# Conv block on one core: where the row chunks, the taps and the sums stand in the convolution stage

## The chip, the core and the metric

The kernel runs on one core of a Trainium2 chip. Its time is the device time in microseconds of one execution; several executions are timed and the median is given. Five engines work in order, each on its own queue of instructions, and wait for each other by semaphores: TensorE (PE; its weight loads are PEld), VectorE (DVE), ScalarE (ACT), GpSimd (POOL) and SyncE (SP), which here issues the DMAs.

## The reference

One layer of a decoder with a convolution mixer, batch 1, T = 256 tokens, D = 2048 channels, an MLP of 8192, all float32.

```python
mod = silu(c) @ mod_w + mod_b                     # 6 vectors of D: sh1, sc1, g1, sh2, sc2, g2
h = rms_norm(x, norm1_g) * (1 + sc1) + sh1
u = h @ w_in + b_in                               # 2048 -> 4096
a, gt = split(u, 2)
u = a * sigmoid(gt)                               # the gate
u = causal_depthwise_conv(u, dw_w, 31 taps) + dw_b
u = silu(layer_norm(u, ln_g, ln_b))
x = x + (1 + g1) * (u @ w_out + b_out)
h = rms_norm(x, norm2_g) * (1 + sc2) + sh2
x = x + (1 + g2) * (square(relu(h @ mlp_w1)) @ mlp_w2)
```

## The kernel before

Channels lie on the 128 partitions, tokens on the free axis: D is KT = 16 tiles of 128 channels by 256 tokens. Every weight of a product is split into a high and a low part (`split_w`: ScalarE writes `hi`, L206, GpSimd or VectorE writes `lo`, L209), and a product is the sum of high x high, high x low and low x high.

**Jobs.** The work of TensorE is a list of jobs: 16 of the input product ("in", one tile of `a` and one of `gt` each), then "out", "up" and "down". The first eight input jobs are computed together while the modulation vectors are loaded and worked out. Jobs 8 to 15 then run one by one: 64 matrix instructions each into a PSUM buffer "mm", of which there are two (job 15 has 96 in another form). These jobs and what stands beside them are the convolution stage, and it is all that the change touches. Per job n in it:

- `evac` (L518 on ScalarE, L519 on VectorE) adds the two halves of the sums; `gate` (L750 sigmoid on ScalarE, L752 on VectorE) writes the gated tile `u[n]`. With that the "mm" buffer is free for a later job.
- *The convolution* of a tile goes one of two ways. Eight tiles (`PE_TILES`) go to TensorE: ScalarE, and for two of them VectorE, makes shifted copies ("wide", L710 and L712), GpSimd a diagonal of taps ("diag", L720), and `pe_conv` issues 32 small matrix instructions (L735) into an "mm" buffer of their own. `CONV_AT` says behind which job which tile comes. The other eight tiles go to VectorE: 31 instructions per tile (L621 to L627, "taps") and a join (L630). `stream` is a generator over all of them that lets the end of one tile's taps alternate with the beginning of the next one's, and `advance(k)` issues the next k steps; `ADVANCE` says how many behind which job.
- *Row chunks.* Part of the modulation comes as rows: `mod_chunk` takes one loaded weight block of 1 MB and issues four matrix instructions (L310) into the PSUM bank "row". Jobs 8 to 12 have four chunks each, job 13 three (`LATE_IN`). `mod_finish` folds a finished row sum into columns (L357) and adds the bias (L348).
- *Shift and sums.* Behind tile 1, `find_shift` (L410, L670) takes a shift from the first two tiles; later tiles start from it and `add_shift` (L674) adds it to the earlier ones. `stats(b)` squares four tiles on ScalarE (L462) and sums them and their squares on TensorE (L680), for the layer norm.

**What sets the order.** The program is written in one sequence, and a scheduler places each engine's instructions by its own estimate of when they are ready, with `urgent()` for those that go first. `tc.issue_after(x)` says that an instruction stands behind x in that order. Loads are issued by `top_up` in a fixed order as buffers come free: seven buffers "raw" hold the blocks of 1 MB of all kinds. In the version before, the row chunks of a job come behind its products and ahead of its convolution tile, the tile behind the last chunk (`step_end`), and nothing orders the next job's products against either. The taps of `advance` are not ordered against the job's gate.

Of the kernel before, what the change touches and what calls it, by code (L numbers as in the profile page):

```python
# [17 lines left out]
KT = D // P  # L18
# [23 lines left out]
FIRST = 4  # L42
PE_TILES = (0, 1, 2, 9, 10, 12, 14, 15)
CONV_AT = {9: (0,), 10: (1,), 11: (2,), 12: (9,), 13: (10,), 14: (12,), 15: (14,)}
ADVANCE = {7: 24, 8: 34, 9: 34, 10: 34, 11: 34, 12: 32, 13: 37, 14: 99}
SHIFT = 2
COPY_AT = {8: 0, 9: 1, 10: 2, 11: 9, 12: 10, 13: 12}
PADDING = 720
# [18 lines left out]
def conv_block(ctx: ExitStack, tc: tile.TileContext, x, vec, dwq, c_row, mod_r, mod_c, w_first, w_in, w_out, w1, w2, out):  # L67
    nc = tc.nc
# [15 lines left out]
    def col(name, j=0, n=1):  # L84
        at = VEC[name] + j
        return v[:, at : at + n]
# [23 lines left out]
    for i in range(2):  # L110
        p = ps.tile([P, 2, 2 * T], F32, name="mm", bufs=2)
# [6 lines left out]
    state = {"used": 0}  # L118
# [12 lines left out]
    def urgent():  # L131
        return tc.high_priority(offset=URGENT)
# [89 lines left out]
    def mm(p, c, key, acts_of, ks=range(KT), merged=False):  # L222
        halves = parts[key]
        for k in ks:
            hi, lo = halves[k // HALF]
            m = acts_of[k // 2][:, k % 2, :]
            if merged:
                out_p, begin, end = p[:, c, 0:T], k == 0, k == KT - 1
                w = hi[:, k % HALF, :]
                nc.tensor.matmul(out_p, w, m[:, 0:T], start=begin, stop=False)  # L230
                nc.tensor.matmul(out_p, w, m[:, T : 2 * T], start=False, stop=False)  # L231
                state["mm_end"] = nc.tensor.matmul(out_p, lo[:, k % HALF, :], m[:, 0:T], start=False, stop=end)  # L232
                continue
            nc.tensor.matmul(p[:, c, :], hi[:, k % HALF, :], m, start=(k == 0), stop=(k == KT - 1))  # L234
            state["mm_end"] = nc.tensor.matmul(  # L235
                p[:, c, T : 2 * T], lo[:, k % HALF, :], m[:, 0:T], start=False, stop=(k == KT - 1),
                skip_group_check=True,
            )
# [101 lines left out]
    def mod_bias(at, n, src):  # L340
        cs = slice(at, at + n)
        which, k = divmod(at, KT)
        if which in amps:
            g = col("n1g" if which == SC1 else "n2g", k, n)
            nc.vector.tensor_tensor(src, src, col("modb", at, n), op=ALU.add)
            nc.vector.tensor_tensor(amps[which][:, k : k + n], src, g, op=ALU.mult)
        else:
            return nc.vector.tensor_tensor(modc[:, cs], src, col("modb", at, n), op=ALU.add)  # L348

    def mod_finish():  # L350
        while pending:
            ats, nj, r = pending.pop(0)
            n = len(ats)
            p = ps.tile([P, 512], F32, name="row", bufs=1)
            with urgent():
                for j in range(nj):
                    state["fold_end"] = nc.tensor.matmul(  # L357
                        p[:, n * j : n * j + n], r[:, j * P : (j + 1) * P], col("pick", 0, n), start=True, stop=True
                    )
                for b, at in enumerate(ats):  # L360
                    with tc.issue_after(state["lo_end"]) if "lo_end" in state else ExitStack():
                        mod_bias(at, nj, p[:, 0 : nj * n].rearrange("p (j n) -> p n j", n=n)[:, b, :])
# [35 lines left out]
    def mods(keys):  # L398
        for key in keys:
            if key[0] == "mod":  # L400
                mod_chunk(*key[1:])
            else:
                mod_col(key[1])
# [28 lines left out]
    def two():  # L432
        return tmp.tile([P, 2, T], F32, name="two", bufs=6)
# [9 lines left out]
    hl = [None] * HALF  # L443
# [34 lines left out]
    for job in jobs:  # L478
        n = quota.get(job, 0)
# [3 lines left out]
        if job[:2] in LATE_GATE:  # L483
            n = LATE_GATE[job[:2]][job[2]]
# [39 lines left out]
    p = ps.tile([P, 512], F32, name="small", bufs=1)  # L524
# [10 lines left out]
    with urgent():  # L535
        part = two()[:, 0, :]
        nc.scalar.activation(part, p[:, 0:T], AF.Copy)
        p = ps.tile([P, 512], F32, name="row", bufs=1)
# [8 lines left out]
    for _ in range(2):  # L547
        p = ps.tile([P, 2, 2 * T], F32, name="mm", bufs=2)
# [31 lines left out]
    for k in range(KT):  # L580
        c = k % 2
# [3 lines left out]
        if c == 0:  # L585
            n = two()
# [20 lines left out]
    def cv(k):  # L607
        return cvs[k // 4][:, k % 4, :]
# [9 lines left out]
    def tap(out, acc, ct, j):  # L618
        s, w = tap_of(ct, j)
        if j == 0:  # L620
            nc.vector.tensor_scalar(out, s, w, col("dwb", ct), op0=ALU.mult, op1=ALU.add)  # L621
        elif acc is None and ct < UNSHIFTED:
            nc.vector.tensor_scalar(out, s, w, None, op0=ALU.mult)
        elif acc is None:
            nc.vector.scalar_tensor_tensor(out, s, w, state["small"][:, T : 2 * T], op0=ALU.mult, op1=ALU.add)
        else:
            nc.vector.scalar_tensor_tensor(out, s, w, acc, op0=ALU.mult, op1=ALU.add)  # L627

    def join(out, acc, s):
        nc.vector.tensor_tensor(out, acc, s, op=ALU.add)  # L630

    def conv_steps(ct):
        acc = ps.tile([P, 2, T], F32, name="acc", bufs=2)
        rest = cp.tile([P, T], F32, name="rest", bufs=2)
        for j in range(TAPS):
            n = j % 2
            tap(rest if j == TAPS - 1 else acc[:, n, :], None if j < 2 else acc[:, n, :], ct, j)
            yield
        join(cv(ct), acc[:, 1, :], rest)

    on_dve = [ct for ct in range(KT) if ct not in PE_TILES]

    def stream():
        tail = iter(())
        for ct in on_dve:
            steps = conv_steps(ct)
            for _ in range((TAPS - 1) // 2):
                next(steps)
                yield
                if next(tail, tail) is not tail:  # L650
                    yield
            for _ in tail:
                yield
            tail = steps
        for _ in tail:
            yield

    conv_taps = stream()

    def advance(n):  # L660
        for _ in range(n):
            next(conv_taps, None)
# [21 lines left out]
    def stats(b):  # L684
        s = squares(cvs[b])
        for k in range(2):
            sum_round([(cv(4 * b + 2 * m + k), s[:, 2 * m + k, :]) for m in range(2)], b == 0 and k == 0)
# [60 lines left out]
    def gate(i, t2):  # L748
        sg = two()[:, 0, :]
        state["sg"] = nc.scalar.activation(sg, t2[:, 1, :], AF.Sigmoid, bias=col("b_in", KT + i))  # L750
        u[i] = ubufs[i % len(ubufs)]
        nc.vector.scalar_tensor_tensor(  # L752
            u[i][:, PAD : PAD + T], t2[:, 0, :], col("b_in", i), sg, op0=ALU.add, op1=ALU.mult
        )
        return sg

    def mix(ct):
# [4 lines left out]
    with urgent():  # L762
# [10 lines left out]
        gate(7, held[7])  # L773
    advance(ADVANCE[HELD - 1])

    for n, job in enumerate(jobs):
# [14 lines left out]
        kind, i = job[0], job[-1]  # L791
        if kind == "out" and i > 0:
            p = ps_two()
        elif not by_tokens(job):
            p = ps.tile([P, 2, 2 * T], F32, name="mm", bufs=2)
# [3 lines left out]
        if job == ("up", 0, 0):  # L799
            mm(p, 0, job + (0,), xa, range(SIDE))  # L800
            for at in range(2 * UNSCALED):
                shift_row(at, shown.pop(("up", 0, at // 2, at % 2)))
            fold_shift()
            mm(p, 0, job + (0,), xa, range(SIDE, KT))
            mm(p, 1, job + (1,), xa)
        elif job in K_OUTER:
            for k2 in range(HALF):
                for c in range(2):
                    mm(p, c, job + (c,), xa if plain else hl, range(2 * k2, 2 * k2 + 2), kind == "out")
        elif kind == "in":  # L810
            rows = [key for key in after[job] if key not in cols_in] if i < KT - 1 else []
            for c in range(2) if i < KT - 1 else (1, 0):
                for ks in (range(HALF), range(HALF, KT)):
                    mm(p, c, job + (c,), hl, ks, i == KT - 1)
            state["step_end"] = state["mm_end"]
            with tc.issue_after(state["mm_end"].ins):
                mods(rows)
            if rows:
                state["step_end"] = state["row_end"]
        elif by_tokens(job):  # L820
            mm_tokens(sums[kind, i // 2], job, u2 if kind == "down" else hl, n == len(jobs) - 1)
        else:
            for c in range(2):
                mm(p, c, job + (c,), hl, merged=kind == "out")
        mod_finish()
        if kind == "in":
# [11 lines left out]
                for key, w in taken:  # L838
                    mod_col(key[1], w)
            for ct in CONV_AT.get(n, ()):  # L840
                with tc.issue_after(state["step_end"].ins):
                    mix(ct)
            advance(ADVANCE.get(n, 0))
            if n == KT - 2:
                with tc.issue_after(state["conv_end"].ins):
                    stats(0)
            if n < KT - 1:
                continue
            sq15 = two()
            with tc.issue_after(state["conv_end"].ins):  # L850
                stats(1)
                stats(2)
            rows = list(after[job])
            with tc.issue_after(state["stats_end"].ins):
# [226 lines left out]
```

## Time and profile before

| | |
|---|---|
| median of 3 runs | 1109.6 us (1109.43 to 1110.14) |
| the profiled execution | 1109.74 us, of which the span in the trace is 1107.9 us |
| mean granted clock of TensorE in it | 0.993 |
| convolution stage, jobs 8 to 15 and their sums | from about 137 to 300 us of the span |
| HBM read and written | 301.15 MB, 12.07 MB |

The page gives busy times and shares of the span, the span in 40 slices with a digit each, the chain of work that ended last, and the costliest groups of instructions. A row of a timeline has the start and the duration in us, the engine, the line of the kernel, the operation, out<-in, the count, and in brackets the engine's idle time before it with what ended it. A row of a window has, behind each engine's busy time, the granted clock, the busy share of DMA and GB/s. A row of the waits has the total time, how often and the longest.

### The profile page before, as it was taken

What the parts mean: (1) busy time and instruction counts of PE and PEld (TensorE: products, weight loads), DVE (VectorE), ACT (ScalarE), POOL (GpSimd) and SP (SyncE); (2) the same over time, 40 slices, a digit from 0 to 9 for tenths busy, and PEclk for the clock granted to TensorE, in tenths of its full rate; (3) what the DMA queues carried; (4) which work ended last, traced back from release to release, by engine and by line L of the source; (5) the groups of instructions that cost most, each with busy time, mean ns of one, the idle gap of its engine ahead of it and who ended that gap; (6) DMA issues with size and microseconds to landing.
All of it is one profiled execution on the core that took longest, in us unless ns stands there. A gap on an engine that the chain in (4) does not pass through costs nothing.

```text
span 1107.9 us, 15389 instructions
## 1 busy us (share of the span) xinstructions
PE 1083.7 (98%) x6018; PEld 892.9 (81%) x6018; DVE 740.6 (67%) x1025; ACT 509.6 (46%) x679; POOL 194.6 (18%) x119
## 2 busy tenths in 40 slices
PE   7999998899999999999999999999999999999998
PEld 4888875677599998888888888888888888888887
DVE  5777789698566976687954667544656565565653
ACT  4111294674586577444444444343444443444431
POOL 0000176558579443000000000000000000000000
PEclk8999999899999999999999999999999999999999
DMA  9999999677799967898986899667888967778621
GB/s 385 420 421 421 417 406 399 257 317 266 276 369 388 414 240 243 250 307 303 405 329 200 231 282 310 239 158 263 250 237 237 251 206 220 226 239 248 209 67 39
DMA packets 142315, 314.23 MB, mean 284 GB/s; under 512 B 87585, under 2 KB 105505, under 8 KB 107297
## 3 DMA queue, kind: packets, MB, share of 16 engines
q1 hardware_dynamic: 142096, 313.11, 80.5%
q8 instruction: 47, 0.77, 0.3%
q14 instruction: 26, 0.21, 0.1%
q10 hardware_dynamic: 146, 0.13, 0.0%
HBM read 301.15 MB, written 12.07 MB: 283 GB/s over the span
## 4 chain that ended last, share of the span: by engine, by line
PE 81%; DMA 10%; DVE 5%; ACT 3%; issue 1%; DVEq 0%; SPq 0%
PE mm L258 20%; PE mm L257 20%; PE mm L259 20%; DMA raw<-mod_c 7%; PE mm L234 4%; DVE acc L627 3%; PE acc L232 2%; PE acc L231 2%; PE acc L230 2%; PE mm L235 2%; DMA first<-w_first 2%; ACT wide L712 1%; PE mm L735 1%; PE row L310 1%; DMA raw<-w_in 1%; DVE raw L390 1%
## 5 line engine op out<-in xcount | busy, mean ns | idle before, releaser
L206 ACT ACTIVATE hi<-raw 128x1024 fp32r<-128x1024 f32 x320 | 335.9, 1058 | 367.7 <-PE mm L259 329.8
L209 DVE TENSOR_TENSOR lo<-raw,hi 128x1024 fp32r<-128x1024 f32 x257 | 313.3, 1223 | 189.3 <-ACT hi L206 188.4
L258 PE MATMUL mm<-lo,u 128*128 128x512 f32 x496 | 193.0, 389 | 0.0
L257 PE MATMUL mm<-hi,u 128*128 128x512 f32 x496 | 193.0, 389 | 0.0
L259 PE MATMUL mm<-hi,u 128*128 128x512 f32 x496 | 192.9, 389 | 0.0
L209 POOL TENSOR_TENSOR lo<-raw,hi 128x1024 fp32r<-128x1024 f32 x63 | 155.9, 2499 | 200.6 <-DMA raw<-w_in 132.3
L259 PE MATMUL mm<-hi,hl 128*128 128x512 f32 x480 | 186.7, 389 | 0.0
L258 PE MATMUL mm<-lo,hl 128*128 128x512 f32 x480 | 186.7, 389 | 0.0
L257 PE MATMUL mm<-hi,hl 128*128 128x512 f32 x480 | 186.7, 389 | 0.0
L390 DVE SCALAR_TENSOR_TENSOR raw<-raw,cond 128x2048 f32<-128x2048 f32 x50 | 116.3, 2328 | 40.3 <-DMA raw<-mod_c 40.3
L259 PEld LDWEIGHTS mm<-hi,u 128*128 128x128 f32 x496 | 93.1, 188 | 19.4
L258 PEld LDWEIGHTS mm<-lo,u 128*128 128x128 f32 x496 | 93.1, 188 | 19.0
L257 PEld LDWEIGHTS mm<-hi,u 128*128 128x128 f32 x496 | 93.1, 188 | 19.0
L258 PEld LDWEIGHTS mm<-lo,hl 128*128 128x128 f32 x480 | 90.1, 188 | 18.7
L257 PEld LDWEIGHTS mm<-hi,hl 128*128 128x128 f32 x480 | 90.1, 188 | 18.7
L259 PEld LDWEIGHTS mm<-hi,hl 128*128 128x128 f32 x480 | 90.1, 188 | 18.7
L627 DVE SCALAR_TENSOR_TENSOR acc<-u,v,acc 128x256 f32<-128x256 f32 x224 | 94.1, 483 | 1.5
L234 PE MATMUL mm<-hl,hi 128*128 128x512 f32 x224 | 82.2, 408 | 5.7 <-DVE u L752 5.7
L562 PE MATMUL mm<-two,first 128*128 128x256 f32 x256 | 60.9, 393 | 8.4 <-ACT two L593 8.4
L235 PE MATMUL mm<-hl,lo 128*128 128x256 f32 x224 | 64.2, 287 | 0.0
L562 PEld LDWEIGHTS mm<-two,first 128*128 128x128 f32 x256 | 49.8, 197 | 17.8 <-ACT two L593 10.8
L232 PE MATMUL acc<-hl,lo 128*128 128x256 f32 x224 | 63.5, 283 | 0.0
(183 smaller groups left out, 1266.8 us busy)
## 6 DMA issues: line engine op xcount, KB each, us to landing
raw<-w SPq DMA_DIRECT2D x128, 1024.0 KB, 5.3
raw<-mod_c SPq DMA_DIRECT2D x62, 1024.0 KB, 11.4
raw<-mod_r SPq DMA_DIRECT2D x32, 1024.0 KB, 8.3
raw<-w_in SPq DMA_DIRECT2D x16, 1024.0 KB, 12.0
raw<-w_out SPq DMA_DIRECT2D x16, 1024.0 KB, 8.1
first<-w_first SPq DMA_DIRECT2D x15, 1024.0 KB, 19.8
flat<-two SPq DMA_DIRECT2D x30, 256.0 KB, 2.7
two<-flat SPq DMA_DIRECT2D x120, 64.0 KB, 4.2
```

Source lines behind the costliest of these rows:

```text
L206: state["w_hi"] = nc.scalar.activation(hi, w[:, ks, :], AF.Copy).ins
L209: end = by.tensor_tensor(lo, w[:, ks, :], hi.bitcast(F32), op=ALU.subtract)
L230: nc.tensor.matmul(out_p, w, m[:, 0:T], start=begin, stop=False)
L232: state["mm_end"] = nc.tensor.matmul(out_p, lo[:, k % HALF, :], m[:, 0:T], start=False, stop=end)
L234: nc.tensor.matmul(p[:, c, :], hi[:, k % HALF, :], m, start=(k == 0), stop=(k == KT - 1))
L235: state["mm_end"] = nc.tensor.matmul(p[:, c, T : 2 * T], lo[:, k % HALF, :], m[:, 0:T], start=False, stop=(k == KT - 1), skip_group_check= ...
L257: nc.tensor.matmul(p, p_hi, hi, start=begin, stop=False)
L258: nc.tensor.matmul(p, p_hi, lo, start=False, stop=False)
L259: nc.tensor.matmul(p, p_lo, hi, start=False, stop=end)
L390: nc.vector.scalar_tensor_tensor(w, w, 1.0, cb, op0=ALU.mult, op1=ALU.mult, accum_out=acc)
L562: step = nc.tensor.matmul(held[n][:, c, :], w[:, 2 * n + c, :], h, start=k == 0 and c == 0, stop=k == KT - 1, skip_group_check=True)
L627: nc.vector.scalar_tensor_tensor(out, s, w, acc, op0=ALU.mult, op1=ALU.add)
```

## The change

Five things, all in the convolution stage:

1. The row chunks of a job with a convolution tile come behind that tile and not ahead of it; the tile now stands behind the job's last product (`mm_end`). The next job's products are ordered behind the last chunk (`rows_end`). Where a job has no tile (job 8), the chunks stay as they were.
2. `mod_finish` is called once more behind the chunks, and the folds of a finished row sum fall among the next products instead of inside a tile.
3. The steps of `advance` are ordered behind the job's gate (`gated`).
4. `ADVANCE` has new numbers, and in `stream` the last tile's taps start only after the tail of the tile before it is done.
5. The sums of the first two groups (`stats(0)`, `stats(1)`) are ordered behind job 14's last product and no longer behind tiles 12 and 14; `stats(2)` stays behind tile 14.

```diff
-ADVANCE = {7: 24, 8: 34, 9: 34, 10: 34, 11: 34, 12: 32, 13: 37, 14: 99}
+ADVANCE = {7: 41, 8: 19, 9: 41, 10: 46, 11: 39, 12: 31, 13: 27, 14: 99}
...
             steps = conv_steps(ct)
+            if ct == on_dve[-1]:
+                for _ in tail:
+                    yield
             for _ in range((TAPS - 1) // 2):
...
-        nc.vector.scalar_tensor_tensor(
+        state["gated"] = nc.vector.scalar_tensor_tensor(
             u[i][:, PAD : PAD + T], t2[:, 0, :], col("b_in", i), sg, op0=ALU.add, op1=ALU.mult
-        )
+        ).ins
...
                 for ks in (range(HALF), range(HALF, KT)):
-                    mm(p, c, job + (c,), hl, ks, i == KT - 1)
-            state["step_end"] = state["mm_end"]
-            with tc.issue_after(state["mm_end"].ins):
-                mods(rows)
-            if rows:
-                state["step_end"] = state["row_end"]
+                    with tc.issue_after(state.pop("rows_end")) if "rows_end" in state else ExitStack():
+                        mm(p, c, job + (c,), hl, ks, i == KT - 1)
+            if not CONV_AT.get(n):
+                with tc.issue_after(state["mm_end"].ins):
+                    mods(rows)
...
             for ct in CONV_AT.get(n, ()):
-                with tc.issue_after(state["step_end"].ins):
+                with tc.issue_after(state["mm_end"].ins):
                     mix(ct)
-            advance(ADVANCE.get(n, 0))
+                with tc.issue_after(state["conv_end"].ins):
+                    mods(rows)
+                if rows:
+                    state["rows_end"] = state["row_end"].ins
+            if rows:
+                mod_finish()
+            with tc.issue_after(state["gated"]):
+                advance(ADVANCE.get(n, 0))
             if n == KT - 2:
-                with tc.issue_after(state["conv_end"].ins):
-                    stats(0)
+                with tc.issue_after(state["mm_end"].ins):
+                    for b in range(2):
+                        stats(b)
...
             with tc.issue_after(state["conv_end"].ins):
-                stats(1)
                 stats(2)
```

## The prediction

> **What bounds the kernel now.** I read the page first, then the list of waits from 130 to 310 us, then the engines' timelines in that stretch, and last the windows with the granted clock.
>
> ```profile
> span 1107.9 us, 15389 instructions
> ...
> PE 1083.7 (98%) x6018; PEld 892.9 (81%) x6018; DVE 740.6 (67%) x1025; ACT 509.6 (46%) x679; POOL 194.6 (18%) x119
> ...
> PE   7999998899999999999999999999999999999998
> ...
> PEclk8999999899999999999999999999999999999999
> ```
>
> TensorE is busy for 98% of the span. What can be gained lies in the few slices of 27.7 us where its digit falls. Behind the first (the loads) the clock digit falls in one alone, the eighth (194 to 222 us), and there and in the slice ahead of it TensorE shows 8 instead of 9: it is the convolution stage (jobs 8 to 15 of the input product). The list of waits in that stage says who waited:
>
> ```profile
> PE mm L234 <- DVE u L752: 5.7, 1, 5.7
> ...
> PE small L680 <- ACT sq L462: 1.3, 1, 1.3
> ```
>
> Columns: total, times, longest. TensorE waited once for 5.7 us, for one gate (L752), and once for 1.3 us, for a square. Here is the first on VectorE, then ScalarE, then TensorE:
>
> ```profile
> 168.13 0.48 DVE L752 SCALAR_TENSOR_TENSOR u<-mm,v,two 128x256 f32<-128x256 f32 x1
> ...
> 171.64 22.02 DVE L627 SCALAR_TENSOR_TENSOR acc<-u,v,acc 128x256 f32<-128x256 f32 x56
> 193.57 0.86 DVE L627 SCALAR_TENSOR_TENSOR rest<-u,v,acc 128x256 f32<-128x256 f32 x2
> 194.36 0.69 DVE L519 TENSOR_TENSOR mm<-mm,two 128x512 f32<-128x512 f32 x1
> 194.96 0.74 DVE L630 TENSOR_TENSOR cv<-acc,rest 128x256 f32<-128x256 f32 x2
> ...
> 196.07 0.47 DVE L752 SCALAR_TENSOR_TENSOR u<-mm,v,two 128x256 f32<-128x256 f32 x1
> ```
> ```profile
> 183.35 0.60 ACT L518 ACTIVATE two<-mm 128x512 f32<-128x512 f32 x1 [1.88 <-PE mm L235]
> 195.08 0.47 ACT L750 ACTIVATE two<-mm,v 128x256 f32<-128x256 f32 x1 [11.13 <-DVE mm L519]
> ```
> ```profile
> 190.26 0.70 PE L410 MATMUL small<-cv,ones 128*128 128x256 f32 x2
> 196.68 0.77 PE L234 MATMUL mm<-hl,hi 128*128 128x512 f32 x1 [5.72 <-DVE u L752]
> ```
>
> Job 10's sums were copied out at 183.35 us, but VectorE stood in an unbroken run of taps and reached the add (L519) only at 194.36. The gate ended at 196.54. Only then was job 10's "mm" buffer free for job 11, and TensorE, done at 190.96, idled. The idling cost more than itself:
>
> ```profile
> 196.60:199.00 2.40, 2.32 (x7) 2.06 (x8) 0.39 (x1) 2.38 (x5) 2.40 (x2) 0.50 0.94 396
> 199.00:201.00 2.00, 2.00 (x7) 1.70 (x7) 0.00 (x0) 1.94 (x6) 2.00 (x1) 0.50 0.14 53
> 201.00:203.00 2.00, 2.00 (x11) 1.68 (x10) 0.00 (x0) 1.95 (x5) 0.29 (x1) 0.81 0.40 57
> 203.00:205.00 2.00, 2.00 (x14) 1.75 (x13) 0.00 (x0) 1.93 (x6) 0.00 (x0) 1.00 0.93 385
> ```
>
> The number after the engines is the granted clock: 0.50 until about 202 us, then 1.00. Lost to it: 2.4 x 0.50 + 2.0 x 0.50 + 2.0 x 0.19 = 2.6 us. So one late gate costs 8.3 us.
>
> **Part 1: taps behind their job's gate, shared out anew.** In the changed program's order, 46 taps and one join stand between job 9's gate and job 10's add, where before there are 64 taps (the 56 and eight around them). A tap in that run takes 22.02 / 56 = 0.393 us; three of the 46 follow a tap of their own tile, and the row of 22 below says that this costs 0.524. After the gate at 168.13 (next instruction 0.39 later) come 46 x 0.393 + 3 x 0.13 + 0.4 = 18.9 us, so the add starts at 187.4. From add to gate it took 1.7 us before (194.36 to 196.07), so the gate ends at about 189.6. TensorE is done at 190.96: the 5.7 us go, with 1.4 us to spare, and with them the 2.6 us of half clock. By hand: -8.3.
>
> What is late next? The following jobs, whose pace on TensorE is:
>
> ```profile
> 216.51 0.99 PE row L357 x8
> ...
> 218.93 0.43 PE mm L234
> ...
> 230.42 3.57 PE row L310 x32
> 233.99 3.45 PE mm L735 x64
> 237.44 0.43 PE mm L234
> ```
> ```profile
> 220.12 2.08 DVE L674 TENSOR_TENSOR cv<-cv,small 128x1024 f32<-128x1024 f32 x2
> ...
> 237.48 11.52 DVE L627 SCALAR_TENSOR_TENSOR acc<-u,v,acc 128x256 f32<-128x256 f32 x22
> ```
>
> A job takes 237.44 - 218.93 = 18.5 us on TensorE: products 11.5, rows 3.6, tile 3.5. On VectorE the changed order has, from gate 10 to gate 11, 40 taps, some ten of them after one of their own tile: 15.7 + 1.3, and about 1.8 for join, add and gate, 18.8 us. From gate 11 to gate 12: 42 taps (16.5), the two additions of the shift (1.9), the four bias additions and a join (0.7), add and gate (1.4), 20.5 us, against 18.5 + 1.0 for the folds (L357), which now stand among job 12's products. So the 1.4 us to spare become 1.1 and then 0.1: gate 12 comes just when job 13's products are due. Gates 13 and 14 have 34 and 28 taps, many of the 0.524 kind, against shorter row blocks, and keep it about level. I take 0.4 us of idling over these three gates; the bounds are 0 and 2 us (0.7 us at each).
>
> **Part 2: row chunks behind the tile, pinned ahead of the next products.** TensorE's instructions are the same; only the seams change. Before: products to rows, rows to tile, tile to products; after: products to tile, tile to rows, rows to products. Three changes of shape per job either way. The seam from tile to rows has no row here; the nearest, tile to fold and fold to tile, lie within the 0.99 us of the eight folds above. I take nothing for it, and 0.2 us either way over five jobs, 1 us, into the range. The two matrix products for the shift (L410) now stand between row chunks, as two seams more; a pair takes 0.70, and I take +0.3 for these. The row buffers come free one tile, 3.5 us, later, so SyncE issues the loads queued behind them later. What covers that: the gates' stage leaves DMA room, as the window below shows (share 0.73), and the weights of a job are loaded a job, 18.5 us, ahead. If that cover were gone, each job would lose up to 3.5 us; I see nothing that asks for it.
>
> ```profile
> 210.00:285.00 75.00, 75.00 (x705) 55.00 (x707) 67.94 (x149) 44.04 (x74) 52.48 (x24) 1.00 0.73 284
> 285.00:300.00 15.00, 13.71 (x178) 6.91 (x170) 5.77 (x12) 7.44 (x17) 2.94 (x3) 1.00 0.82 287
> 310.00:400.00 90.00, 89.97 (x751) 89.77 (x750) 66.20 (x95) 59.97 (x89) 57.50 (x32) 1.00 0.92 370
> ```
>
> The added order (next products only after the row block) makes all of a job's products stand behind its chunks; but TensorE runs in order, and the chunks' loads now have 3.5 us more to land, so nothing that waits today waits longer.
>
> **Part 3: sums among products.** The statistics of the first two groups go in behind job 14's and among job 15's products; only the third stays behind tile 14. Its square moves too:
>
> ```profile
> 287.81 1.06 ACT L462 ACTIVATE sq<-cv 128x1024 f32<-128x1024 f32 x1
> ```
>
> It was queued on ScalarE behind the copies for tile 15. In the changed order it stands between two splits ahead of gate 15, since the last VectorE tile is finished a job sooner. Job 15's products lie between and cover it. So TensorE's wait of 1.3 us goes; if the square were late by as much as today, nothing would be gained, so 0 is the other bound. What comes next in that place, the squares of tiles 12 to 15, is unchanged.
>
> **The rest.** From 310 us TensorE is full (89.97 of 90 us) and its order is the same, so what is gained earlier stays gained; DMA at 0.92 there shifts along with the buffers it fills.
>
> **The sum.** -5.7 - 2.6 - 1.3 + 0.4 + 0.3 = -8.9 us. The profiled execution took 1109.74 us (span 1107.9 and 1.84 around it), 0.14 over the median of 1109.6. So 1109.74 - 8.9 = 1100.8 for a run like it, and 1100.7 for the median. A measurement of this kernel can tell about 0.2%, 2.2 us, from no change.
>
> **The rivals.**
>
> A. A tight gate slips: the margins at gates 12 to 14 are worked out as 0.1 us, and if VectorE is 3% slower than my rows over the 100 us that five jobs take, it is 3 us late at one of them, and the half clock comes back once: 1100.7 + 3 + 2.6 - 0.4 = 1105.9; a lateness of 1.5 us without the clock gives 1101.8. For it: VectorE is busy 67.94 of 75 us there. Against it: the tap rows repeat within 1%. Chance 0.13.
>
> B. The clock drops at every small idling. Three short waits at gates 12 to 14 would each bring 2.6 us of half clock, 7.8 in all, with 1 us of waits: 1100.7 + 8.8 - 0.4 = 1109.1, no change. Against it: in 285 to 300 us TensorE idled 1.3 us at once and the clock row still says 1.00. [...] Chance 0.04.
>
> C. Slower: the taps pay the price of the slow kind. The changed stream finishes each tile's tail apart at its end, and a tap behind one of its own tile takes 0.524 us instead of 0.393. From gate 9 on there are some 190 taps; about 55 are counted as slow already. If the other 135 were too, that is 135 x 0.131 = 17.7 us more on VectorE, each us of which TensorE waits for beyond 1.4 us to spare: 1100.7 + 17.7 - 1.4 = 1117.0, or more with the clock. It makes the kernel slower than before once more than some 95 of them pay (8.9 + 2.2 + 1.4 over 0.131). Against it: in the changed order two tiles still alternate through most of jobs 10 to 12. Chance 0.05.
>
> D. The change does not do what it says: the gates could still stand behind too many taps. The built order shows 46 and not 64, so 0.01.
>
> **How the numbers follow.** My forecast has 0.77: 1100.7, from 1099.0 (no new wait, no seams for the shift, the others 1 us cheaper) to 1104.6 (2 us of waits, seams 1 us dearer, the square still waited for) with all at their ends at once. Range for 8 in 10: 1098.5 to 1104.0, the lower end 0.5 under the forecast's for the spread of the runs (1109.43 to 1110.14), the upper one with the milder half of A in it. Faster by over 0.2%: forecast, A and a little of B, 0.91; within 0.2%: 0.04; slower: 0.05.
>
> **What would show it.** Right: no wait of TensorE for L752 above 1 us; the clock at 1.00 from 150 to 300 us; the add of job 10 near 187.4 and its gate near 189.1 us; no wait before the statistics; the output products some 9 us earlier; the rest of the trace the same, shifted. Wrong: a wait for a gate of jobs 11 to 14 over 2 us, a clock of 0.50 anywhere in the stage, or runs of taps at 0.52 us where two tiles should alternate.

## The result, and the profile after

The changed kernel takes 1100.93 us (median of 6 runs, 1100.61 to 1101.12), the kernel before 1109.72 us beside it (6 runs, 1109.41 to 1110.14): 8.8 us less, ratio 0.992, 95% interval 0.9907 to 0.9933. The forecast was 1100.7, with 1098.5 to 1104.0 as its range.

The page of the changed kernel, its span, its engines, and the digits of TensorE and of its granted clock by slices of 27.5 us:

```profile
span 1099.1 us, 15389 instructions
...
PE 1081.8 (98%) x6018; PEld 891.9 (81%) x6018; DVE 746.9 (68%) x1025; ACT 510.5 (46%) x679; POOL 192.7 (18%) x119
...
PE   7999999999999999999999999999999999999998
...
PEclk8999999999999999999999999999999999999999
```

The two slices with an 8 and the lower clock digit behind the loads are gone. TensorE's list of waits from 130 to 310 us (total, times, longest) is now, in full:

```profile
PE mm L231 <- DVE hl L220: 1.0, 2, 0.7
PE mm L230 <- ACT hl L217: 0.5, 1, 0.5
```

Neither the gate (now L755) nor the square (for L683) is in it. Both lines belong to the products behind the stage, and the kernel before has them with the same numbers. VectorE's timeline of the changed kernel, at job 10's add (L519) and gate and at the next two gates:

```profile
187.47 0.69 DVE L519 TENSOR_TENSOR mm<-mm,two 128x512 f32<-128x512 f32 x1
188.71 0.49 DVE L755 SCALAR_TENSOR_TENSOR u<-mm,v,two 128x256 f32<-128x256 f32 x1 [0.54 <-ACT two L753]
...
207.68 0.48 DVE L755 SCALAR_TENSOR_TENSOR u<-mm,v,two 128x256 f32<-128x256 f32 x1
...
228.18 0.48 DVE L755 SCALAR_TENSOR_TENSOR u<-mm,v,two 128x256 f32<-128x256 f32 x1
```

and TensorE's, with a tile, the two sums for the shift (L410) between the row chunks (L310), and the start of the products of job 11 (L234 at 191.77) and job 13:

```profile
183.22 3.66 PE L738 MATMUL mm<-wide,diag 128*32 128x256 f32 x64
186.81 0.70 PE L410 MATMUL small<-cv,ones 128*128 128x256 f32 x2
187.44 2.78 PE L310 MATMUL row<-raw,cz 128*32 128x512 f32 x24
190.15 0.70 PE L410 MATMUL small<-cv,ones 128*128 128x256 f32 x2
190.78 1.06 PE L310 MATMUL row<-raw,cz 128*32 128x512 f32 x8
191.77 0.50 PE L234 MATMUL mm<-hl,hi 128*128 128x512 f32 x1
...
203.27 3.66 PE L738 MATMUL mm<-wide,diag 128*32 128x256 f32 x64
...
229.66 0.50 PE L234 MATMUL mm<-hl,hi 128*128 128x512 f32 x1
```

Job 10's gate ends at 189.20 and job 11 starts at 191.77 without a wait: 2.6 us to spare. Job 12's gate ends at 228.66 and job 13 starts at 229.66: 1.0 us to spare. The windows give the granted clock behind the place where it used to fall (the number after the engines):

```profile
194.00:196.00 2.00, 2.00 (x14) 1.72 (x13) 1.86 (x5) 1.95 (x5) 0.00 (x0) 1.00 0.96 406
196.00:198.00 2.00, 2.00 (x13) 1.76 (x12) 1.86 (x5) 1.98 (x4) 0.45 (x1) 1.00 1.05 442
```

### The profile page after: what moved, and what is told of

It reads as the page before. It is cut to its first block, busy times and chain, and to the rows that moved or that the text cites. A ratio compares the mean times of both kernels' runs of the same rounds, so it can differ in the third digit from the quotient of the medians.

```text
span 1099.1 us, 15389 instructions
## 1 busy us (share of the span) xinstructions
PE 1081.8 (98%) x6018; PEld 891.9 (81%) x6018; DVE 746.9 (68%) x1025; ACT 510.5 (46%) x679; POOL 192.7 (18%) x119
## 4 chain that ended last, share of the span: by engine, by line
PE 88%; DMA 10%; DVE 2%; ACT 1%; issue 0%; SPq 0%; ACTq 0%
PE mm L258 20%; PE mm L257 20%; PE mm L259 20%; DMA raw<-mod_c 9%; PE mm L234 6%; PE mm L235 3%; PE acc L232 2%; PE acc L230 2%; PE acc L231 2%; PE mm L738 2%; PE row L310 2%; DVE raw L390 1%; PE mm L231 1%; DMA x<-x 1%; PE mm L232 1%; PE mm L230 1%
## 5 line engine op out<-in xcount | busy, mean ns | idle before, releaser
L627 DVE SCALAR_TENSOR_TENSOR acc<-u,v,acc 128x256 f32<-128x256 f32 x224 | 96.8, 486 | 2.2
L234 PE MATMUL mm<-hl,hi 128*128 128x512 f32 x224 | 80.3, 401 | 0.0
L231 PE MATMUL acc<-hl,hi 128*128 128x256 f32 x224 | 63.4, 283 | 0.0
```

## The experiments

The trace says that the wait and the half clock went. It does not say which part of the change took them away, nor whether the half clock came from the wait. The first eight runs take the change apart; the last four keep TensorE busy during the wait. Kernels of one group ran beside the same runs of the kernel before; between groups its median moves by 0.7 us (1109.84, 1109.17 and 1109.50), so tenths are compared within a group only.

| group | kernel | median (us) | lowest to highest | less than before, same group |
|---|---|---|---|---|
| 1 | taps part alone | 1101.55 | 1101.42 to 1101.76 | 8.3 |
| 1 | row part alone | 1102.08 | 1101.88 to 1102.16 | 7.8 |
| 1 | sums part alone | 1108.35 | 1107.73 to 1108.85 | 1.5 |
| 1 | changed, old shares | 1104.84 | 1103.48 to 1105.10 | 5.0 |
| 2 | changed, again | 1100.96 | 1100.84 to 1101.13 | 8.2 |
| 2 | changed, no sums part | 1101.96 | 1101.81 to 1102.37 | 7.2 |
| 2 | changed, no row part | 1100.54 | 1100.29 to 1100.64 | 8.6 |
| 2 | changed, no order on the taps | 1101.02 | 1100.76 to 1101.04 | 8.2 |
| 3 | before, 24 fillers | 1112.08 | 1111.93 to 1112.69 | -2.6 |
| 3 | before, 18 fillers | 1114.98 | 1112.25 to 1115.12 | -5.5 |
| 3 | before, 12 fillers | 1114.19 | 1113.59 to 1114.71 | -4.7 |
| 3 | before, 6 fillers | 1109.77 | 1109.48 to 1109.94 | -0.3 |

**The taps part alone.** The kernel before with three edits:

```diff
-ADVANCE = {7: 24, 8: 34, 9: 34, 10: 34, 11: 34, 12: 32, 13: 37, 14: 99}
+ADVANCE = {7: 41, 8: 19, 9: 41, 10: 46, 11: 39, 12: 31, 13: 27, 14: 99}
...
+            if ct == on_dve[-1]:
+                for _ in tail:
+                    yield
...
-            advance(ADVANCE.get(n, 0))
+            with tc.issue_after(state["gated"]):
+                advance(ADVANCE.get(n, 0))
```

> The kernel before with the taps part alone (new shares, taps ordered behind the gate, tails apart); row chunks and sums as before. Theory 1 (the forecast's: this part alone moves job 10's add ahead of the end of TensorE's work): 46 taps stand ahead of that add, no wait for the gate at job 11, granted clock 1.00 from 194 to 205 us, 1.3 us wait for the square left: 1109.7 - 8.3 + 0.4 (idling at later gates) = 1101.8. Theory 2 (either part alone does it, since each takes the same run of taps apart): the same, 1101.4 to 1102.2. Theory 3 (the taps part needs the row part: with rows ahead of the tile the gate's inputs come at another time, and a wait comes up elsewhere): 1104 or more, with a wait of TensorE for a gate of 2 us or more.

Measured: 1101.55. First two rows of the kernel before that the prediction did not need, the tile ahead of job 11 and the row block behind it, then the same two of this run, with job 11's first product between them:

```profile
186.70 3.63 PE L735 MATMUL mm<-wide,diag 128*32 128x256 f32 x64
...
210.71 3.64 PE L310 MATMUL row<-raw,cz 128*32 128x512 f32 x32
```
```profile
186.64 3.64 PE L738 MATMUL mm<-wide,diag 128*32 128x256 f32 x64
...
190.55 0.58 PE L234 MATMUL mm<-hl,hi 128*128 128x512 f32 x1
...
202.50 3.64 PE L310 MATMUL row<-raw,cz 128*32 128x512 f32 x32
```

Between them stand the same instructions in the same kind of order. They took 210.71 - 186.70 = 24.01 us before and 202.50 - 186.64 = 15.86 now, 8.15 less. Job 11's products, with one sum for the shift among them in both kernels, took 210.71 - 196.68 = 14.03 us before and 202.50 - 190.55 = 11.95 now: 2.1 of half clock. The other 6.1 are the way from the tile to the first product (9.98 before, 3.91 now): the wait's 5.72 and 0.35 more, since without a wait the first product starts 0.35 us ahead of the end that the trace gives for the sum before it (190.55 against 190.20 + 0.70). In this run's list of waits the gate is gone and the square is left:

```profile
PE small L683 <- ACT sq L462: 1.3, 1, 1.3
```

Theory 3 falls. Theories 1 and 2 need the next run.

**The row part alone.** The kernel before with the edits to rows, tiles, `rows_end` and `mod_finish`; no line that issues a tap is touched, and the shares are the old ones:

```diff
-                    mm(p, c, job + (c,), hl, ks, i == KT - 1)
-            state["step_end"] = state["mm_end"]
-            with tc.issue_after(state["mm_end"].ins):
-                mods(rows)
...
+                    with tc.issue_after(state.pop("rows_end")) if "rows_end" in state else ExitStack():
+                        mm(p, c, job + (c,), hl, ks, i == KT - 1)
...
+                with tc.issue_after(state["conv_end"].ins):
+                    mods(rows)
```

> The kernel before with the row part alone (row chunks behind the tile, pinned ahead of the next products); taps and sums as before. In its built order 47 taps and three joins stand ahead of job 10's add, without any order on the taps. Theory 1 (the forecast's: this part is worth nothing by itself, +0.3 for the seams and up to 1 either way): 1109.7 to 1111. Theory 2 (either part alone takes the run of taps apart): no wait for the gate at job 11, clock 1.00 there, 1.3 us wait for the square left: 1101.4 to 1102.4. Theory 3 (partly: the gate comes earlier but the joins delay it, and TensorE waits 1 to 3 us): 1103 to 1107.

Measured: 1102.08, which is theory 2; the forecast's theory, under which this part is worth nothing, misses by 7.6 us at its nearer end. VectorE's timeline of this run, from job 9's gate to job 10's add:

```profile
168.13 0.48 DVE L752 SCALAR_TENSOR_TENSOR u<-mm,v,two 128x256 f32<-128x256 f32 x1
...
171.65 16.14 DVE L627 SCALAR_TENSOR_TENSOR acc<-u,v,acc 128x256 f32<-128x256 f32 x41
187.70 0.69 DVE L519 TENSOR_TENSOR mm<-mm,two 128x512 f32<-128x512 f32 x1
```

The gate stands at 168.13 in the kernel before too, and there the run of taps that starts at 171.64 is 56 long; here it is 41, so that 47 taps stand ahead of the add instead of 64, and it comes at 187.70 instead of 194.36. (The timeline shows two joins ahead of the add, not the three of the expectation.) The scheduler, given other places for chunks and tiles on TensorE, put fewer taps ahead of the add by itself. Which of its estimates moved was not tried.

**The sums part alone.**

```diff
             if n == KT - 2:
-                with tc.issue_after(state["conv_end"].ins):
-                    stats(0)
+                with tc.issue_after(state["mm_end"].ins):
+                    for b in range(2):
+                        stats(b)
...
-                stats(1)
                 stats(2)
```

> The kernel before with the sums part alone (statistics of the first two groups among the last products). The wait for the gate at job 11 and the half clock behind it stay. Theory 1 (forecast): the 1.3 us wait for the square goes, 1108.4. Rival (the wait moves to the third group's square or to the next statistics): 1109.4 to 1109.9. Rival 2 (the sums among the products cost seams of their own): 1108.8 or more although the wait is gone.

Measured: 1108.35, ratio 0.9987, interval 0.9978 to 0.9996. The first two lines of its list of waits: the gate's stays and the square's, which stood second, is gone, as in theory 1:

```profile
PE mm L234 <- DVE u L752: 5.7, 1, 5.7
PE mm L231 <- DVE hl L220: 1.0, 2, 0.7
```

**The changed kernel with the old shares.** Only the line `ADVANCE` is as before.

> The changed kernel with the old shares of taps (24, 34, 34, 34, 34, 32, 37) in place of the new ones; all else as changed. Theory A (the shares set how many taps stand ahead of each gate): 34 instead of the new counts, gates 10 to 12 come earlier but taps pile up ahead of the later gates 13 and 14, with a wait of 1 us or more there: 1102 to 1105. Theory B (the order alone decides, the shares hardly matter, since VectorE takes the taps that are ready as it goes): 1100.5 to 1101.5, no wait for a gate.

Measured: 1104.84, as theory A has it in size, but at another gate than it says. The add of job 10 is early (188.10), the gates of jobs 11 to 14 too, and then VectorE waits for work. Its timeline at the adds of jobs 13 and 14 and at the last gate, and TensorE's at tile 15 (L738, from the copies L715):

```profile
241.98 0.70 DVE L519 TENSOR_TENSOR mm<-mm,two 128x512 f32<-128x512 f32 x1 [3.61 <-ACT two L518]
...
260.53 0.70 DVE L519 TENSOR_TENSOR mm<-mm,two 128x512 f32<-128x512 f32 x1 [0.76 <-ACT two L518]
...
282.14 0.47 DVE L755 SCALAR_TENSOR_TENSOR u<-mm,v,two 128x256 f32<-128x256 f32 x1
```
```profile
285.92 5.35 PE L738 MATMUL acc<-wide,diag 128*32 128x256 f32 x64 [2.40 <-ACT wide L715]
```

The order holds back what VectorE could have done in those idle 3.61 us; what the shares leave over stands ahead of job 15's gate, which comes at 282.14 instead of 278.02. TensorE waits 2.40 us for the copies, and the windows show the clock at 0.50 behind it:

```profile
286.00:287.00 1.00, 1.00 (x16) 0.67 (x19) 0.01 (x1) 0.98 (x4) 0.00 (x0) 0.64 1.00 418
287.00:288.00 1.00, 1.00 (x16) 0.65 (x12) 0.00 (x0) 1.00 (x1) 0.00 (x0) 0.50 1.04 434
288.00:289.00 1.00, 1.00 (x13) 0.57 (x9) 0.00 (x0) 0.33 (x2) 0.00 (x0) 0.50 0.98 410
289.00:290.00 1.00, 1.00 (x17) 0.69 (x13) 0.00 (x0) 0.00 (x0) 0.00 (x0) 0.65 1.04 442
```

A window at 0.64 was at 0.50 for 0.72 of its 1 us, one at 0.65 for 0.70: 0.72 + 1 + 1 + 0.70 = 3.42 us at 0.50, which is 1.7 lost at most. With the 2.4 of the wait that is 4.1, and this kernel is 3.9 us over the changed one (1100.93 and 1100.96 in two other groups). Of its four runs three took 1104.63 to 1105.10 us at a mean granted clock of 0.995 over the execution; the fourth took 1103.48 at 1.000. So the clock did not fall at all in that run, and it is 2.5 us over the changed kernel, about the wait alone; that its wait was the same is not shown, since it was not the traced one. This is the mechanism of the prediction's rival A, at a gate for which it was not worked out.

**The changed kernel again, and without one part at a time.**

> The changed kernel again, as the measure for the three beside it: 1100.9, within 0.3.

Measured: 1100.96. Without the sums part (the kernel's sums as before, all else as changed):

> The changed kernel without its sums part (statistics of the first two groups where they stood before). Theory 1: the wait for the square of 1.3 us is back and nothing else differs, so the sums part is worth 1.3 to 1.5 beside the others as it was alone: 1102.3. Rival (with the gates early the sums part is worth nothing, or the last gate comes so late that the wait is hidden): 1100.9 to 1101.2.

Measured: 1101.96, 1.0 us more than the changed kernel beside it: the sums part is worth 1.0 beside the others, where the wait that it removes is 1.3. Theory 1, though 0.3 short. Without the row part (the taps and sums parts on the kernel before):

> The changed kernel without its row part (row chunks ahead of the tile as before, not pinned). Theory 1 (the row part is worth nothing once the taps are apart, and costs 0.3 to 0.8 in seams): 1100.1 to 1100.6. Rival 1 (the row part is needed with the sums part, a wait for a gate or a square comes back): 1102 or more. Rival 2 (row and taps parts are equal and overlap entirely, no seams): 1100.9.

Measured: 1100.54, below the changed kernel's lowest run with all its runs. So the row part costs 0.4 us where the taps part stands. TensorE's timeline of this run, the row block, the tile, the first sum and the first product of job 11, then the row block behind its products, and job 13's first product:

```profile
183.11 3.64 PE L310 MATMUL row<-raw,cz 128*32 128x512 f32 x32
186.56 3.64 PE L738 MATMUL mm<-wide,diag 128*32 128x256 f32 x64
190.13 0.70 PE L410 MATMUL small<-cv,ones 128*128 128x256 f32 x2
190.48 0.58 PE L234 MATMUL mm<-hl,hi 128*128 128x512 f32 x1
...
202.43 3.64 PE L310 MATMUL row<-raw,cz 128*32 128x512 f32 x32
...
229.10 0.50 PE L234 MATMUL mm<-hl,hi 128*128 128x512 f32 x1
```

From the end of job 10's products to that of job 11's it took 202.43 - 183.11 = 19.32 us, and in the changed kernel 203.27 - 183.22 = 20.05: 0.73 more for the same instructions. What differs is the seams. In the changed kernel each sum for the shift stands alone between blocks of another shape, and what follows starts 0.63 us behind the sum's start (187.44 - 186.81 and 190.78 - 190.15). Here the first takes 0.35 (190.48 - 190.13), and the second, among the products, lengthens them from 11.50 to 11.95 us: 0.46 of the 0.73. Another 0.25 is the row block that the second sum cuts in two: 2.71 + 0.99 us against 186.56 - 183.11 = 3.45. From there to job 13's start it took 26.67, and in the changed kernel 26.39: 0.28 less, with the folds among products rather than inside a tile. Together 0.45.

Without `issue_after(state["gated"])` around `advance`, all else as changed, new shares included:

> The changed kernel with its new shares but without ordering the taps behind the gate. In its built order 47 taps and three joins stand ahead of job 10's add. Theory A (the shares were made for the order, as the run with the old shares and the order showed; without the order they matter little): 1100.7 to 1101.2, no wait for a gate, clock 1.00. Theory B (the order is what brings the gates forward): the add of job 10 comes later than 190 us and TensorE waits 2 us or more, 1104 or more.

Measured: 1101.02, the changed kernel's time. Its add of job 10:

```profile
187.62 0.69 DVE L519 TENSOR_TENSOR mm<-mm,two 128x512 f32<-128x512 f32 x1
```

Theory A. With the rows moved and the new shares the order on the taps does nothing; with the old shares the order is there and 3.9 us are lost.

**Does the half clock come from the wait?** The kernel before, with N matrix products whose result is not used ("fillers") behind job 10's tile and ahead of the first sum for the shift, into the bank of that sum, and job 11's products ordered behind them:

```diff
+        for _ in range(24):
+            with tc.issue_after(state["conv_end"].ins):
+                state["conv_end"] = nc.tensor.matmul(p, ones, cv(0), start=True, stop=True)
+        state["filled"] = state["conv_end"].ins
...
+                    with tc.issue_after(state.pop("filled")) if "filled" in state else ExitStack():
+                        mm(p, c, job + (c,), hl, ks, i == KT - 1)
```

> The kernel before with 24 more matrix products of 0.3 us, whose result is not used, behind job 10's first shift sum, and job 11's products ordered behind them: TensorE has no idling of over 1 us while it waits for job 10's gate. Job 11 starts as late as before, or 0 to 2 us later, and the shift comes late (a wait of about 3.2 us at the folds), so the whole is slower than before in any case. Theory 1 (the idling itself brings the half clock): granted clock 1.00 from 190 to 205 us, about 1109.7 - 2.6 + 4.9 = 1112.0. Rival (the clock falls with a late start of products, whatever TensorE does ahead of it): 0.50 for some us, 1113.5 or more.

Measured: 1112.08. TensorE's timeline (fillers, first product of job 11, row block behind) and two windows of the stretch in which the kernel before has 0.50:

```profile
190.35 10.63 PE L669 MATMUL small<-cv,ones 128*128 128x256 f32 x48
...
201.50 0.58 PE L234 MATMUL mm<-hl,hi 128*128 128x512 f32 x1
...
213.08 3.64 PE L310 MATMUL row<-raw,cz 128*32 128x512 f32 x32
```
```profile
196.00:197.00 1.00, 1.00 (x7) 0.87 (x6) 1.00 (x3) 1.00 (x2) 0.32 (x1) 1.00 1.09 459
198.00:199.00 1.00, 1.00 (x6) 0.88 (x5) 0.00 (x0) 0.98 (x3) 1.00 (x2) 1.00 0.82 344
```

Job 11 starts 4.8 us later than before, yet the clock stays at 1.00 through all of it (in every window from 189 to 207 us): the half clock comes from the idling, and the rival falls. Job 11's products take 213.08 - 201.50 = 11.58 us here, with both sums for the shift ahead of them, against 14.03 in the kernel before and 11.95 with the taps part alone, each with one sum among them. A filler takes 10.63 / 24 = 0.44 us, and not the 0.3 of the expectations, so the next three doses left less idling at this place than they say. They ask what length of idling brings the clock down: 1.3 us in the kernel before had not, 2.40 us with the old shares had.

> As the run with 24, with 18: the same order on TensorE, with an idling of about 1.9 us. [...] Rival (any idling of over 1.5 us drops it): 0.50 for 3.4 us, 1.7 us more than with 24.

Measured: 1114.98, in five runs 1112.25, 1113.11 and three near 1115.0. At job 11 no idling is left, and the clock holds (1.00 in every window from 189 to 207 us). But job 11 now starts 2.6 us earlier than with 24 fillers, and TensorE waits at the folds (L357), where it did not with 24. Its timeline there, and one window of 0.50 out of 218.7 to 225.5:

```profile
218.75 1.87 PE L357 MATMUL row<-v,rowsb 128*128 128x4 f32 x8 [2.68 <-ACT rowsb L317]
```
```profile
222.00:223.00 1.00, 1.00 (x16) 0.23 (x8) 1.00 (x8) 0.00 (x0) 0.00 (x0) 0.50 0.95 401
```

So it says nothing on 1.9 us of idling, which it was made for, and something else: a start 2.6 us earlier is paid back at the folds, and the idling of 2.68 us costs 2.9 us on top in the usual run, the half clock alone. The mean granted clock of the execution is lowest in the three runs near 1115.0, at 0.994; it is 0.998 at 1113.11 and 0.996 at 1112.25.

> As the run with 24, with 12: the same order, with an idling of about 3.7 us. [...] Rival (only an idling as long as 5.7 us drops it): the same time as with 24, clock 1.00.

Measured: 1114.19. TensorE's two waits in it and a window behind each:

```profile
198.03 0.70 PE L410 MATMUL small<-cv,ones 128*128 128x256 f32 x2 [1.82 <-ACT cv L747]
...
218.86 1.06 PE L357 MATMUL row<-v,rowsb 128*128 128x4 f32 x8 [3.11 <-ACT rowsb L317]
```
```profile
199.00:200.00 1.00, 1.00 (x8) 0.86 (x7) 0.00 (x0) 0.98 (x3) 1.00 (x2) 1.00 0.33 139
...
221.00:222.00 1.00, 1.00 (x16) 0.34 (x8) 1.00 (x3) 0.00 (x0) 0.00 (x0) 0.50 1.07 451
```

1.82 us of idling did not bring the clock down (1.00 in every window from 196 to 207 us), 3.11 us did (0.50 for 3.4 us), and the kernel takes 2.1 us more than with 24. So the rival falls, though at the folds and not at the place that the run was made for.

> As the run with 24, with 6: an idling of about 4.0 us ahead of job 11, whose products start with the second shift sum among them, as before. [...] Rival: clock 1.00, 1109.7.

Measured: 1109.77, though the clock does fall (0.50 from 197.2 to 200.6, behind a wait of 2.85 us at job 11, where 4.0 was expected). The time is the rival's, the clock is not. Job 11 starts at 196.68, exactly as before, and its products are through 0.6 us earlier (row block at 210.13 instead of 210.71); a wait of 0.56 us at the folds gives it back.

## Why the prediction was right, and where it was not

| term | forecast | measured | from |
|---|---|---|---|
| wait for the gate of job 10 | -5.7 | -6.1 | 9.98 - 3.91, taps part alone |
| half clock behind it | -2.6 | -2.1 | 14.03 - 11.95, taps part alone |
| wait for the square | -1.3 | -1.0 | 1101.96 to 1100.96 |
| idling at gates 12 to 14 | +0.4 | 0 | no such wait |
| seams | +0.3 | +0.4 | 1100.54 to 1100.96 |
| sum | -8.9 | -8.8 | the whole: 1109.72 - 1100.93 = 8.8 |

The terms come from different groups of runs and each is good to a few tenths, so that they meet the whole to 0.1 is partly luck.

- **The late gate.** Right to 0.1 us: the add at 187.4 forecast, 187.47 measured. From gate to gate VectorE took 18.97 and 20.50 us, forecast 18.8 and 20.5.
- **The margins.** Too small by 1.2 us at job 11 (1.4 forecast, 2.6 measured), and by 0.9 at job 13, so the idling of 0.4 did not come. The step that failed is the starting point: the gate follows the add by 1.24 us and not 1.7, because the two joins and the tap that stood between them (L630 and L621) stand elsewhere now, and TensorE is at job 11 at 191.77 and not 190.96, because the second sum for the shift now stands ahead of its products too, and the seams around the sums are dearer than the 0.3 taken for them. The paces that follow were right.
- **The half clock.** Right in kind, shown by the fillers; 0.5 too large, in part since the products did not take twice their time at 0.50 (a pair took 0.64 us in the kernel before, against 0.35 at 1.00). The wait was 0.35 too small, so the 8.3 of the two together came out as 8.15.
- **Part 1 and Part 2.** The sum is right, its attribution is not. The prediction put the whole 8.3 down to the taps part and nothing to the row part. Each alone removes the wait (1101.55 and 1102.08), so they do not add. The step that failed is "TensorE's instructions are the same; only the seams change": it looked at the engine that the part touches, and not at what the scheduler then does on VectorE. Had only the row part been made, the forecast would have been wrong by 7.6 us.
- **"Shared out anew".** With the rows moved, the new shares matter only with the order: the old ones cost 3.9 us with it (1104.84), and without it, in the row part alone, which also leaves the sums as they were and the tails together, TensorE waited neither for a gate nor for copies. Whether the order or the shares do the work in the taps part alone was not tried. Where the prediction counted the gates of jobs 11 to 14, the old shares fail at job 15's.
- **Rival B** (half clock at every small idling) had no idling at the gates to act on; the three waits behind the stage that the changed kernel's list does have, 0.7 us at most, left the clock at 1.00. In the traced runs single waits of 1.3 us (the kernel before) and 1.82 us (12 fillers) in this stage left the clock at 1.00, and single waits of 2.40 us (old shares) to 5.72 us (the kernel before) brought it down.
- **Rival C** (slow taps) acted in part: VectorE's busy time rose from 740.6 to 746.9 us, but only 2.7 of the 6.3 are taps (L627 into `acc`, 94.1 to 96.8 us), of the 17.7 that the rival takes, and the time to spare at the gates covered them. Another 3.0 are the copies for two tiles (L710, now L713, 9.6 to 12.6), for which the second trace of the changed kernel has rows of 5.51 and 4.26 us, the first 7.78 and 5.07, and the kernel before 4.79 and 5.12.

Of the versions run, the changed kernel without its row part is the fastest: 1100.54 against 1100.96, less than the 0.2% bound of a comparison with before, but with no overlap of the runs.

## What to carry to other kernels

When one late instruction on an off-path engine holds a buffer, find it by what stands between its inputs and itself on its own queue, and price the clock that falls with the wait along with the wait (here 2.1 us for a wait of 5.72). Where a scheduler lays out the order, read the order of every engine for each part of a change alone before saying which part does it: here two parts each did the whole, and one of them cost 0.4 us for nothing. An order that holds work back needs shares that fill every gap; with the old shares here, the rest came due at the last gate.

## What the runs showed of the hardware

The stretches at half clock in the convolution stage were of two lengths. The granted clock was at 0.50 from 194.92 to 201.75 us in the kernel before (6.83), from 286.28 to 289.70 with the old shares (3.42), and from 197.18 to 200.60 with 6 fillers (3.42); with 18 fillers it was 6.8 and with 12 it was 3.4, each worked out from the share of the window in which it turns. In the traced runs single idlings of 2.40 us (old shares), 2.68 (18 fillers), 2.85 (6 fillers), 3.11 (12 fillers) and 5.72 (the kernel before) brought it down, and 1.3 (the kernel before) and 1.82 (12 fillers) did not. The length of the stretch did not go by that of the idling: 6.8 us with 2.68 of idling, 3.4 with 2.85 and with 3.11. The length of the idling alone does not seem to decide whether the clock falls either: with the old shares, where the trace has the 2.40 us, the mean granted clock was 0.995 in three runs and 1.000 in the fourth, and the kernel with 18 fillers, whose trace has one idling of 2.68 us, gave 1112.25 in one run and near 1115.0 in three. Only one run of each was traced, so that the others had the same idling is not shown, and neither is what made them differ.
